# Inverting 8x8 blocks on VectorE, five weight remainders by accumulating DMA, and inputs laid out by transfer

## The chip, the cores and the metric

The kernel runs on one core of one Trainium2 chip. The metric is the device time of one execution in microseconds; the kernel before takes 667.52 us, the median of 3 runs (667.09 to 667.53).

## The reference

Two decoder layers on 256 tokens of width 1024, and a final RMSNorm, all in float32. Layer 0 has a mixer with one input projection, whose columns go to a gated-DeltaNet part (8 heads of 64, with a causal convolution of width 4 and SiLU on q, k, v) and to a short gated convolution part (512 channels, `y = Bg * conv3(Cg * h)`); one output projection follows, then a squared-ReLU MLP of width 4096. Layer 1 has a sparse attention mixer and the same kind of MLP. Every sublayer begins with an RMSNorm.

The delta rule works on chunks of 64 tokens. What matters here is its triangular solve:

```python
m_low = jnp.where(strict, jnp.einsum('nbhik,nbhjk->nbhij', kb, kc) * decay, 0.0)
a_mat = m_low + jnp.eye(c, dtype=f32)
u = lax.linalg.triangular_solve(a_mat, vc * bc[..., None], left_side=True, lower=True, unit_diagonal=True)
w = lax.linalg.triangular_solve(a_mat, kb * jnp.exp(gc)[..., None], left_side=True, lower=True, unit_diagonal=True)
```

So for each head and each chunk of 64 tokens the inverse of a 64x64 unit lower triangular matrix is wanted.

## The kernel before, in words

**Order.** The instructions of each engine stand in a fixed order, written out when the kernel is built. The class `Order` (from line 166) runs all parts of the kernel as generators ("streams") against a list of costs for each operation; whichever stream could start first, and on a tie has the lower priority number, emits next. Each engine and the DMA queue (`SP`) then execute their lists in order, with semaphores between them. Eight PSUM banks are handed out by the same planner; the projections (`MAIN`, priority 9) take a bank only when two are free. When operations are added, taken away or moved, the whole order behind them is planned anew.

**Weights.** Projections run at full float32 accuracy by splitting each weight into a rounded part and a remainder, and each activation likewise, with three float32r matmuls for one product (`mm256`). Weights come in units of up to 128x1024. `loads` (line 491) issues all transfers from memory on SP's queue into eight staging slots (`st`); `splits` (line 511) makes of unit i the rounded part `uh` on ScalarE and the remainder `ul = st - uh` on VectorE, each into one of four buffers (`UB = 4`). For the units listed in `BYDMA` (line 37), ScalarE instead writes `-uh` into `ul`, and GpSimd issues a DMA that adds `st` to it (`refill`, line 534); the planner counts 4500 ns for its landing (`DLAT`). The units are numbered: 0 to 7 for K, 8 to 15 for z and the decay inputs, 16 to 19 V, 20 to 23 Q, 24 to 27 CG (the gate Cg), 28 to 31 h, 32 to 35 Bg, 36 to 43 the output projection of layer 0.

**Layer 0.** TensorE runs the projections in that order; a group of four column blocks accumulates in PSUM and is read when its time comes: K and V through a convolution on VectorE, Q through one on GpSimd (`pool_conv`), CG after GpSimd has made `r2` (the row scale squared, `cg_evac`), h through a second convolution on GpSimd. Meanwhile `chain_k` computes the norms of k and calls `invert` (line 1271).

**The inversion.** Tokens stand in two chunks `c` of 128, that is, four blocks of 32 tokens on the partitions, for 8 heads. `prepare(c)` computes `al` (the lower triangle with its sign changed, transposed: 128 x 8 heads x 128). From it `prepare` transposes the four 32x32 diagonal blocks to `lc`, masks the entries of 2-blocks into `tt`, adds the identity, and transposes that to `uc`: the inverses of the 2x2 blocks. `invert` then doubles the block size in four levels (2, 4, 8, 16; masks in `lvl`). A level has `left` (128 matmuls of 32x32 from `al` and `tt`), a product with the mask to `ys` on VectorE, `right` (128 matmuls from `uc` and `ys`), an addition to `tt` and a transpose to `uc` on VectorE:

```python
for l in range(1, 5):
    bs, blocks = yield from left(0)
    ...
    bs = yield from right(blocks)
```

A last step of another form joins 32-blocks to 64-blocks (`U64`). Then `chain_main` solves, and `output` leads to `ya`, the half of the output projection's input that comes from the heads; `yb` is the half from the short convolution.

**The front.** `loads` issues first the 40 columns of norm weights (`wn`, 160 bytes on each partition), then x in five pieces between the first weight pieces, and later the other parameters (`par`, before weight piece 8). x and the parameters stand in memory row by row, one row per partition; each transfer takes a part of every row. The first RMSNorm (`start`, line 909) waits for a piece of x and for `wn`.

Of the kernel before, what the change touches and what calls it, by code (L numbers as in the profile page):

```python
# [20 lines left out]
T = 256  # L21
KT = D // 128
FF = 4096
NEG = -1e30
EPS = 1e-6
CH = 4096
UN = 1024
XBIAS, DBIAS, XB0 = 300, -400, 1e9
GM, GT, GO = 2, 1, 1
HEAD, CL = 0, 0  # L30
STORE, GST = (0, 2, 4, 6, 7, 8), (2,)
FIRST, XS = (1,) * 8, ((1, 2), (2, 4), (4, 6), (6, 8))
PK, PW, PR, F1, GZ, ZP, LD, RT, P2 = 1, 1, 1, 1, 1, 1, 1, 21, 8
KPOOL, VPOOL, QPOOL, CVB = (), (), (0, 1, 2, 3), {'conv': 4, 'pool': 2}
TAP = {'V': 290}
CHAIN, EARLY, TOK_FIRST = 0, 16, False
BYDMA, DLAT = (*range(113, 121, 2), *range(129, 141, 2)), 4500
YIELD = (0.0, 0.0, 0.0)
TICK, BUSY = 10240 / 3, 1500.0
FULL, DRAIN, BARE, STAY, LEAVE = (128, 128), 0.0, 0.0, 0.0, 0.0  # L40
# [20 lines left out]
    return [(UN // 2, FIRST), (528, (1,) * 8)] + [w] * 7 + [w] * 16 + l1 + [w] * 16  # L61


def _layout(i):

    ev = i['ev_w_in'][0]
    od = i['od_w_in'][0]
# [41 lines left out]
    for k in ORDER1:  # L109
# [3 lines left out]
    par = {}  # L113
    col = lambda v: v.reshape(-1, 128).T
    rep = lambda v: np.broadcast_to(v.reshape(1, -1), (128, v.size))
    par['wn'] = np.concatenate([col(v) for v in (i['mix_norm'][0], i['mlp_norm'][0], i['mix_norm'][1],
                                                 i['mlp_norm'][1], i['final_norm'])], axis=1)
# [7 lines left out]
    par['strict'] = (r[:, None] > r[None, :])  # L125
    b, c = np.arange(128) % 32, np.arange(32)
    par['lvl'] = np.concatenate([((b[:, None] // s) % 2 == 1) & (c[None, :] // s == b[:, None] // s - 1)
                                 for s in (1, 2, 4, 8, 16)], axis=1)
    par['i32'] = b[:, None] == c[None, :]
    par['onorm'] = rep(i['ev_o_norm'][0])  # L130
    par['sctap'] = i['ev_sc_conv'][0].reshape(3, 4, 128).transpose(2, 1, 0).reshape(128, 12)
    inv = np.float32(500000.0) ** (-np.arange(0, 16, 2, dtype=np.float32) / np.float32(16))
# [15 lines left out]
    for k, v in par.items():  # L148
# [1 line left out]
        off[k] = (o, v.shape[1])  # L150
        o += v.shape[1]
        parts.append(v)
    xt = i['x'][0].reshape(T, KT, 128).transpose(2, 1, 0).reshape(128, KT * T)
# [7 lines left out]
    return c32(np.concatenate(flat)), c32(xt), c32(np.concatenate(parts, axis=1)), off  # L161

# [3 lines left out]
class Order:  # L166
# [29 lines left out]
    def flag(self, name):  # L196
        self.flags.setdefault(name, self._now())
# [212 lines left out]
def _build(ctx, nc, tc, wts, xin, parin, out, off):  # L410
# [15 lines left out]

    npar = off['rc'][0]
    par = const.tile([128, npar], F32, name="par")
    X = e.X = const.tile([128, KT, T], F32, name="X")
    e.rtab = const.tile([128, 2, T], F32, name="rtab")  # L430
    ones = const.tile([128, 1], F32, name="ones")

    e.zeros = const.tile([128, 512], BF16, name="zeros")

    def keep(bank):
# [44 lines left out]
    def get(dst, src, k, name):  # L480
# [2 lines left out]
        order.spend('D', k * 512 / 330)  # L483
        flag(name)

    def load_x(a, b):
        yield from get(X[:, a:b], xin[:, a * T:b * T].rearrange("p (k t) -> p k t", t=T), (b - a) * T, f'x{a}')
        for m in range(a + 1, b):
            flag(f'x{m}')

    def loads():
        cut = off['ident'][0]
        before = {P2: [get(par[:, cut:], parin[:, cut:npar], npar - cut, 'par2')],
                  RT: [get(e.rtab, parin[:, npar:].rearrange("p (a t) -> p a t", a=2), 2 * T, 'rtab')]}
        for p, x in zip((1, 2, 3, 4), XS):
            before[p] = [load_x(*x)]
        head = [get(par[:, :cut], parin[:, :cut], cut, 'par'), load_x(0, 1)]
        before[HEAD] = head + before.get(HEAD, [])
        for p, (pos, k) in enumerate(pieces):
            for g in before.get(p, ()):  # L500
                yield from g
            slot, o = place[p]
            if not o:
                if slot >= SB:
                    yield 'flag', f'st{slot - SB}'
                st = stage.tile([128, UN], F32, name="st")
            staged[p] = st[:, o:]
            yield from get(st[:, o:o + k], bass.AP(tensor=wts.tensor, offset=wts.offset + pos, ap=[[k, 128], [1, k]]),
                           k, f'ld{p}')

    def splits(first):
        for i in range(first, len(units), 2):
# [278 lines left out]
    class Norm:  # L791


        def __init__(self, idx, last=False):
            self.idx, self.last = idx, last
            self.w = par[:, off['wn'][0] + 8 * idx:off['wn'][0] + 8 * idx + 8]
            self.x = self.acc = None
            self.begun = self.count = self.sums = 0

# [100 lines left out]
    def main():  # L900
        n0 = Norm(0)

        def root():

            yield 'flag', 'norm3'
            yield 'A'
            A.activation(tmp.tile([128, 1], F32, name="tb", bufs=3), ones, AF.Sqrt)

        def start(m):
            yield 'flag', f'x{m}'  # L910
            yield 'flag', 'par'
# [24 lines left out]
        for i, (a, b) in enumerate(zip(STORE, STORE[1:])):  # L936
            spawn(store(i, a, b))
# [55 lines left out]
def layer0(e, n, nxt):  # L993
# [4 lines left out]
    with ExitStack() as ctx:  # L998
# [253 lines left out]
        def prepare(c):  # L1252

            al = AL[c]
            yield from keys(c)
            yield from scores(c, KB, al)
            tt, lc, uc, ys = (p1.tile([128, 8, 32], F32, name=f"{k}{c}", tag=f"lz{c}" if k == "lc" else f"{k}{c}")
                              for k in ("tt", "lc", "uc", "ys"))
            yield 'V'
            for b in range(4):  # L1260
                r = slice(32 * b, 32 * b + 32)
                V.transpose(lc[r], al[r, :, r])
            V.tensor_mul(tt, lc, b32(lvl[:, 0]))
            V.tensor_add(tt, tt, b32(P('i32')))
            V.transpose(uc, tt)
            parts[c] = al, tt, uc, ys
            flag(f'parts{c}')

        parts = [None, None]

        def invert():
# [2 lines left out]
                spawn(prepare(c))  # L1274
            for c in range(2):
                yield 'flag', f'parts{c}'

            def left(shift):
                bs = yield from banks(2)
# [18 lines left out]
                                      start=True, stop=True, tile_position=(i, i))  # L1298
                return bs

            for l in range(1, 5):
                bs, blocks = yield from left(0)
                yield 'V'
                for c in range(2):
                    V.tensor_mul(parts[c][3], view(bs[c], 8, 32), b32(lvl[:, l]))
                    release(bs[c])
                bs = yield from right(blocks)
                yield 'V'
                for c in range(2):
# [777 lines left out]
```

## Time and profile before

| | |
|---|---|
| median of 3 runs | 667.52 us |
| the profiled execution's own time | 666.4 us |
| its span, first to last instruction | 664.6 us |
| mean granted TensorE clock | 0.991 |
| TensorE matmuls busy | 646.4 us (97%), 6642 instructions |
| VectorE busy | 474.0 us (71%), 911 |
| ScalarE busy | 375.4 us (56%), 715 |
| GpSimd busy | 127.5 us (19%), 167 |

PE is TensorE's matmuls, PEld its weight loads, DVE VectorE, ACT ScalarE, POOL GpSimd, SP the queue that issues transfers. Times in rows are in us from the start of the span, mean durations of one instruction in ns. Matmuls overlap each other, so the sum of their durations is more than their time; the distance between starts tells what one costs. Nearly all instructions carry the line of a helper (329), so groups are told apart by their tiles: `b` is a PSUM bank, `x` the normed input, `uh` and `ul` a weight unit's two parts, `st` its staging slot. A bracket at the end of a row holds the time for which the engine stood idle before it, and what ended that.

### The profile page before, as it was taken

To read this page: it belongs to the slowest core of one execution; us is meant where nothing else is said; L and a number is where in the kernel's file an instruction comes from. 1 tells how busy PE (TensorE), PEld (TensorE's weight loads), DVE (VectorE), ACT (ScalarE), POOL (GpSimd) and SP (SyncE) were. 2 spreads that over 40 slices of the span, in tenths; PEclk is the share of its full clock that TensorE was granted. 3 is DMA by queue.
4 is the path that set the end of the run, shared out by engine and by line. 5 is a ranking of instruction groups with operands and counts; after the bars stand their busy time and mean duration, and the time that the engine had idled before them with its cause. 6 is when DMAs were issued, how large, how long until landed. Compare 5 with 4: busy or idle time off the path is not lost.

```text
span 664.6 us, 16204 instructions
## 1 busy us (share of the span) xinstructions
PE 646.4 (97%) x6642; PEld 621.1 (93%) x6644; DVE 474.0 (71%) x911; ACT 375.4 (56%) x715; POOL 127.5 (19%) x167
## 2 busy tenths in 40 slices
PE   8999989999999999999999999999999999999995
PEld 6999878999999999999999887898999999999994
DVE  5999868876887776555557998986778777545441
ACT  7566223344676665444447689888567666544430
POOL 1101696300200000111124433120220000012121
PEclk8999989999999999999999999999999999999998
DMA  8862433245566666666667659552656555555401
GB/s 289 309 225 83 135 101 97 64 125 163 177 200 193 191 193 196 195 193 197 196 185 165 199 179 321 147 156 67 184 184 204 192 192 190 193 194 196 148 1 65
DMA packets 33915, 114.34 MB, mean 172 GB/s; under 512 B 3888, under 2 KB 4400, under 8 KB 33840
## 3 DMA queue, kind: packets, MB, share of 16 engines
q1 hardware_dynamic: 32112, 107.66, 50.8%
q0 software_dynamic: 1440, 5.24, 4.1%
q8 instruction: 52, 0.85, 0.5%
q10 hardware_dynamic: 288, 0.39, 0.2%
q14 instruction: 23, 0.19, 0.1%
HBM read 106.99 MB, written 1.05 MB: 163 GB/s over the span
## 4 chain that ended last, share of the span: by engine, by line
PE 83%; DVE 9%; ACT 2%; issue 2%; DMA 2%; SPq 0%; POOLq 0%; DVEq 0%; ACTq 0%
PE b L329 83%; DVE ul L329 3%; DVE cvconv L329 2%; ACT uh L329 1%; DMA X<-xt 1%; DMA ul<-st 1%; DVE rqt L329 1%; DVE al L329 1%; DVE lc L329 1%; ACT ul L329 0%; DVE preconv L329 0%; SPq L482 0%; DVE r L329 0%; DVE kst L329 0%; DVE tt L329 0%
## 5 line engine op out<-in xcount | busy, mean ns | idle before, releaser
L329 ACT ACTIVATE uh<-st 128x1024 fp32r<-128x1024 f32 (+3 forms) x204 | 206.2, 1012 | 205.4 <-PE b L329 170.9
L329 DVE TENSOR_TENSOR ul<-st,uh 128x1024 fp32r<-128x1024 f32 (+3 forms) x194 | 229.5, 1185 | 118.0 <-ACT uh L329 117.5
L329 PE MATMUL b<-x,uh 128*128 128x256 f32 x1664 | 294.7, 281 | 1.8 <-ACT uh L329 1.4
L329 PEld LDWEIGHTS b<-x,uh 128*128 128x128 f32 x1664 | 253.3, 189 | 3.8 <-ACT uh L329 1.9
L329 PE MATMUL b<-x,ul 128*128 128x256 f32 x832 | 232.3, 279 | 2.2 <-DVE ul L329 0.9
L329 PE MATMUL b<-U,uh 128*128 128x256 f32 x1024 | 174.2, 276 | 0.0
L329 PEld LDWEIGHTS b<-x,ul 128*128 128x128 f32 x832 | 157.5, 189 | 3.6 <-DVE ul L329 1.8
L329 PEld LDWEIGHTS b<-U,uh 128*128 128x128 f32 x1024 | 154.1, 188 | 0.0
L329 PE MATMUL b<-U,ul 128*128 128x256 f32 x512 | 141.3, 276 | 0.0
L329 PEld LDWEIGHTS b<-U,ul 128*128 128x128 f32 x512 | 96.1, 188 | 0.0
L329 POOL TENSOR_TENSOR nacc<-nacc,sq 128x256 f32<-128x256 f32 x24 | 32.0, 1334 | 234.4 <-ACT sq L329 224.8
L329 DVE SCALAR_TENSOR_TENSOR t<-b,rbc 128x256 f32<-128x256 f32 x64 | 26.6, 423 | 8.3 <-PE b L329 8.3
L329 ACT ACTIVATE U<-u 128x256 fp32r<-128x256 f32 x64 | 26.8, 419 | 2.0
L329 ACT ACTIVATE px<-b,nm 128x256 f32<-128x256 f32 (+1 forms) x64 | 26.3, 423 | 2.0 <-DVE nm L329 1.7
L329 DVE TENSOR_TENSOR U<-u,U 128x256 fp32r<-128x256 f32 x64 | 26.5, 419 | 0.0
L329 ACT ACTIVATE u<-t 128x256 f32<-128x256 f32 x64 | 25.6, 401 | 0.0
L329 DVE TENSOR_TENSOR X<-X,b 128x256 f32<-128x256 f32 (+1 forms) x28 | 13.9, 514 | 16.3 <-PE b L329 16.3
L329 POOL TENSOR_TENSOR X<-X,par 128x256 f32<-128x256 f32 x8 | 5.6, 702 | 100.3 <-ACT nacc L329 91.7
L329 PE MATMUL b<-uh,x 128*128 128x264 f32 (+1 forms) x128 | 24.7, 289 | 0.0
L329 PE MATMUL b<-ohl,uh 128*128 128x256 f32 x128 | 23.9, 287 | 0.2
L329 PEld LDWEIGHTS b<-uh,x 128*128 128x128 f32 x128 | 20.3, 188 | 0.2 <-issue 0.2
L329 PEld LDWEIGHTS b<-ohl,uh 128*128 128x128 f32 x128 | 19.6, 188 | 0.7 <-ACT ohl L329 0.3
(276 smaller groups left out, 772.3 us busy)
## 6 DMA issues: line engine op xcount, KB each, us to landing
st<-wts SPq DMA_DIRECT2D x188, 512.0 KB, 4.1
ul<-st POOLq DMA_DIRECT2D x10, 512.0 KB, 5.1
st<-wts SPq DMA_DIRECT2D x8, 280.0 KB, 3.3
st<-wts SPq DMA_DIRECT2D x8, 264.0 KB, 5.9
st<-wts SPq DMA_DIRECT2D x8, 256.0 KB, 6.3
X<-xt SPq DMA_DIRECT2D x3, 256.0 KB, 6.3
par<-par SPq DMA_DIRECT2D x1, 525.0 KB, 5.8
out_dram<-X SPq DMA_DIRECT2D x2, 256.0 KB, 2.8
```

The lines of the kernel that those rows point to most:

```text
L329: r = f(*a, **k)
```

## The change

**Inversion.** The mask table `lvl` keeps only levels 8 and 16. `prepare` no longer transposes and masks for 2-blocks; it multiplies the four 32x32 blocks of `al` by a mask of the upper part of 8-blocks (`up8`) and sums over the four block columns to `W8`, so that each row holds its 8 entries within its own 8-block. When both chunks are there, `eights` runs a substitution on VectorE over 16 heads at once: six steps, each a shuffle that brings row i of every 8-block to all its rows, a product and an addition; then it adds the identity, spreads the 8 columns to 32 with the mask `own8` into `uc`, and transposes to `tt`. Levels 8 and 16 and all behind them are as before.

**Remainders.** Units 21, 23, 25, 27 and 29 are added to `BYDMA`.

**Inputs.** x, with `wn` in front of its first piece, and the two parts of the parameters are stored so that each transfer reads one contiguous range. The norm weights come with the first piece of x (296 columns), their own transfer falls away, and `start` does not wait for it. A tile `gap0` keeps the addresses of the others.

```diff
-BYDMA, DLAT = (*range(113, 121, 2), *range(129, 141, 2)), 4500
+BYDMA, DLAT = (*range(21, 31, 2), *range(113, 121, 2), *range(129, 141, 2)), 4500
...
+def xcuts():
+    return [(0, WN + T)] + [(WN + a * T, WN + b * T) for a, b in XS]
...
-                                 for s in (1, 2, 4, 8, 16)], axis=1)
-    par['i32'] = b[:, None] == c[None, :]
+                                 for s in (8, 16)], axis=1)
+    own = b[:, None] // 8 == c[None, :] // 8
+    par['own8'] = own
+    par['up8'] = own & (c[None, :] > b[:, None])
+    par['i8'] = b[:, None] % 8 == c[None, :8]
...
+    def rows(src, at, n):
+        return bass.AP(tensor=src.tensor, offset=src.offset + 128 * at, ap=[[n, 128], [1, n]])
     def load_x(a, b):
-        yield from get(X[:, a:b], xin[:, a * T:b * T].rearrange("p (k t) -> p k t", t=T), (b - a) * T, f'x{a}')
-        for m in range(a + 1, b):
+        yield from get(xw[:, a:b], rows(xin, a, b - a), b - a, f'x{max(0, a - WN) // T}')
+        for m in range((a - WN) // T + 1, (b - WN) // T):
             flag(f'x{m}')
...
-        head = [get(par[:, :cut], parin[:, :cut], cut, 'par'), load_x(0, 1)]
-        before[HEAD] = head + before.get(HEAD, [])
...
         def start(m):
             yield 'flag', f'x{m}'
-            yield 'flag', 'par'
...
             for b in range(4):
                 r = slice(32 * b, 32 * b + 32)
-                V.transpose(lc[r], al[r, :, r])
-            V.tensor_mul(tt, lc, b32(lvl[:, 0]))
-            V.tensor_add(tt, tt, b32(P('i32')))
-            V.transpose(uc, tt)
+                V.tensor_mul(md[r], al[r, :, r], P('up8')[r, None, :].to_broadcast([32, 8, 32]))
+            V.tensor_reduce(W8[:, c], md.rearrange("p h (b c) -> p h c b", c=8), axis=AX.X, op=OP.add)
...
+        def eights():
+            W = W8.rearrange("p c h i -> p (c h) i")
+            for i in range(6, 0, -1):
+                yield 'V'
+                B = p2.tile([128, 16, 8], F32, name="b8")[:, :, i + 1:]
+                V.stream_shuffle(B, W[:, :, i + 1:], [p // 8 * 8 + i for p in range(32)])
+                V.tensor_mul(B, B, W[:, :, i:i + 1].to_broadcast([128, 16, 7 - i]))
+                V.tensor_add(W[:, :, i + 1:], W[:, :, i + 1:], B)
+            yield 'V'
+            V.tensor_add(W, W, P('i8')[:, None, :].to_broadcast([128, 16, 8]))
+            for c in range(2):
+                yield 'V'
+                _, tt, uc, _ = parts[c]
+                V.tensor_mul(uc.rearrange("p h (b i) -> p h b i", i=8), W8[:, c, :, None, :].to_broadcast([128, 8, 4, 8]),
+                             P('own8').rearrange("p (b i) -> p b i", i=8)[:, None].to_broadcast([128, 8, 4, 8]))
+                V.transpose(tt, uc)
...
+            yield from eights()
...
-            for l in range(1, 5):
+            for l in range(2):
```

More of the change, by code (lines that the diff above doesn't have):

```diff
@@ L24 @@
 NEG = -1e30
+WN = 40
 EPS = 1e-6
@@ L29 @@
 GM, GT, GO = 2, 1, 1
-HEAD, CL = 0, 0
+CL = 0
 STORE, GST = (0, 2, 4, 6, 7, 8), (2,)
@@ L115, in _layout @@
     rep = lambda v: np.broadcast_to(v.reshape(1, -1), (128, v.size))
-    par['wn'] = np.concatenate([col(v) for v in (i['mix_norm'][0], i['mlp_norm'][0], i['mix_norm'][1],
-                                                 i['mlp_norm'][1], i['final_norm'])], axis=1)
+    wn = np.concatenate([col(v) for v in (i['mix_norm'][0], i['mlp_norm'][0], i['mix_norm'][1],
+                                          i['mlp_norm'][1], i['final_norm'])], axis=1)
     par['ident'] = np.eye(128)
@@ L152, in _layout @@
         parts.append(v)
-    xt = i['x'][0].reshape(T, KT, 128).transpose(2, 1, 0).reshape(128, KT * T)
+    xt = np.concatenate([wn, i['x'][0].reshape(T, KT, 128).transpose(2, 1, 0).reshape(128, KT * T)], axis=1)
+    xt = [np.ravel(xt[:, a:b]) for a, b in xcuts()]
     c32 = lambda a: np.ascontiguousarray(a, dtype=np.float32)
@@ L160, in _layout @@
             c = c[:, k:]
-    return c32(np.concatenate(flat)), c32(xt), c32(np.concatenate(parts, axis=1)), off
+    par = np.concatenate(parts, axis=1)
+    o = off['rc'][0]
+    par = np.concatenate([np.ravel(par[:, :o]), np.ravel(par[:, o:])])
+    return c32(np.concatenate(flat)), c32(np.concatenate(xt)), c32(par), off
 class Order:
@@ L428, in _build @@
     par = const.tile([128, npar], F32, name="par")
-    X = e.X = const.tile([128, KT, T], F32, name="X")
+    xw = const.tile([128, WN + KT * T], F32, name="X")
+    X = e.X = xw[:, WN:].rearrange("p (k t) -> p k t", t=T)
     e.rtab = const.tile([128, 2, T], F32, name="rtab")
     ones = const.tile([128, 1], F32, name="ones")
+    const.tile([128, 56], F32, name="gap0")
     e.zeros = const.tile([128, 512], BF16, name="zeros")
@@ L484, in get @@
         flag(name)
+    def rows(src, at, n):
+        return bass.AP(tensor=src.tensor, offset=src.offset + 128 * at, ap=[[n, 128], [1, n]])
     def load_x(a, b):
-        yield from get(X[:, a:b], xin[:, a * T:b * T].rearrange("p (k t) -> p k t", t=T), (b - a) * T, f'x{a}')
-        for m in range(a + 1, b):
+        yield from get(xw[:, a:b], rows(xin, a, b - a), b - a, f'x{max(0, a - WN) // T}')
+        for m in range((a - WN) // T + 1, (b - WN) // T):
             flag(f'x{m}')
     def loads():
[L492 to L495, printed above, removed]
+        before = {P2: [get(par, rows(parin, 0, npar), npar, 'par2')],
+                  RT: [get(e.rtab.rearrange("p a t -> p (a t)"), rows(parin, npar, 2 * T), 2 * T, 'rtab')]}
+        for p, x in enumerate(xcuts()):
             before[p] = [load_x(*x)]
-        head = [get(par[:, :cut], parin[:, :cut], cut, 'par'), load_x(0, 1)]
-        before[HEAD] = head + before.get(HEAD, [])
         for p, (pos, k) in enumerate(pieces):
@@ L507, in loads @@
             staged[p] = st[:, o:]
-            yield from get(st[:, o:o + k], bass.AP(tensor=wts.tensor, offset=wts.offset + pos, ap=[[k, 128], [1, k]]),
-                           k, f'ld{p}')
+            yield from get(st[:, o:o + k], rows(wts, pos // 128, k), k, f'ld{p}')
     def splits(first):
@@ L795, in __init__ @@
             self.idx, self.last = idx, last
-            self.w = par[:, off['wn'][0] + 8 * idx:off['wn'][0] + 8 * idx + 8]
+            self.w = xw[:, 8 * idx:8 * idx + 8]
             self.x = self.acc = None
@@ L1256, in prepare @@
             yield from scores(c, KB, al)
-            tt, lc, uc, ys = (p1.tile([128, 8, 32], F32, name=f"{k}{c}", tag=f"lz{c}" if k == "lc" else f"{k}{c}")
-                              for k in ("tt", "lc", "uc", "ys"))
+            tt, md, uc, ys = (p1.tile([128, 8, 32], F32, name=f"{k}{c}", tag=f"lz{c}" if k == "md" else f"{k}{c}")
+                              for k in ("tt", "md", "uc", "ys"))
             yield 'V'
@@ L1261, in prepare @@
                 r = slice(32 * b, 32 * b + 32)
-                V.transpose(lc[r], al[r, :, r])
-            V.tensor_mul(tt, lc, b32(lvl[:, 0]))
-            V.tensor_add(tt, tt, b32(P('i32')))
-            V.transpose(uc, tt)
+                V.tensor_mul(md[r], al[r, :, r], P('up8')[r, None, :].to_broadcast([32, 8, 32]))
+            V.tensor_reduce(W8[:, c], md.rearrange("p h (b c) -> p h c b", c=8), axis=AX.X, op=OP.add)
             parts[c] = al, tt, uc, ys
             flag(f'parts{c}')
+        W8 = small("w8", 2, 8, 8)
+        def eights():
[14 more added lines that the diff above has]
+                V.transpose(tt, uc)
         parts = [None, None]
```

## The prediction

> **What bounds the kernel now.** I read the page's busy times first, then the chain that ended last, then busy time by stretch.
>
> ```profile
> span 664.6 us, 16204 instructions
> PE 646.4 (97%) x6642; PEld 621.1 (93%) x6644; DVE 474.0 (71%) x911; ACT 375.4 (56%) x715; POOL 127.5 (19%) x167
> ...
> PE 83%; DVE 9%; ACT 2%; issue 2%; DMA 2%; SPq 0%; POOLq 0%; DVEq 0%; ACTq 0%
> ```
>
> TensorE is busy 97% of the span and carries 83% of the chain, so time is gained where TensorE has less to do, stands still, or runs at a lower clock. The change lies in layer 0, ahead of the MLP that begins at 176.9 us (last row, from the chain in order of time). Its stretches (columns: PE, PEld, DVE, ACT, POOL busy with instructions; granted clock; DMA share, GB/s):
>
> ```profile
> 5.30:9.20 3.90, 3.57 (x25) 2.97 (x24) 2.16 (x4) 1.71 (x5) 0.00 (x0) 1.00 0.87 256
> 9.20:10.50 1.30, 0.00 (x0) 0.00 (x0) 0.88 (x2) 1.30 (x4) 0.00 (x0) 1.00 1.06 407
> 10.50:15.00 4.50, 4.24 (x20) 4.04 (x21) 4.38 (x10) 4.50 (x12) 0.00 (x0) 0.62 1.04 405
> ...
> 54.70:68.60 13.90, 13.90 (x128) 13.77 (x131) 13.61 (x35) 7.20 (x10) 2.15 (x2) 1.00 0.37 106
> 68.60:106.50 37.90, 34.32 (x1202) 32.17 (x1202) 28.72 (x55) 10.21 (x16) 32.13 (x41) 0.95 0.38 118
> 106.50:141.60 35.10, 34.01 (x495) 31.79 (x495) 27.94 (x66) 12.00 (x21) 10.46 (x14) 1.00 0.26 77
> ...
> 176.88 175.68 PE b L329 x1547
> ```
>
> Up to 68.6 us VectorE is almost full (13.61 of 13.90) but TensorE is full too, so VectorE costs nothing there. From 68.6 to 106.5, where the inversion runs, TensorE loses 37.90 - 34.32 = 3.6 us standing still, and the clock of 0.95 takes 5% of 37.9, about 1.9 us. After that it is nearly full again. The MLP and layer 1 behind are untouched, so what layer 0 gives goes to the end one for one.
>
> **The inversion on TensorE.** Each of four levels issues two batches of 128 small matmuls (2 chunks x 8 heads x 4 blocks):
>
> ```profile
> 68.53 1.31 PE L329 MATMUL b<-tt,al 32*32 32x32 f32 x128
> 69.77 0.50 PE L329 MATMUL b<-x,uh 128*128 128x256 f32 x2
> ...
> 72.56 1.31 PE L329 MATMUL b<-ys,uc 32*32 32x32 f32 x128 [1.10 <-DVE ys L329]
> ...
> 84.12 1.54 PE L329 MATMUL b<-tt,al 32*32 32x32 f32 x128
> ...
> 92.19 0.25 PE L329 MATMUL b<-ys,uc 32*32 32x32 f32 x4 [1.78 <-issue]
> ```
>
> From the start of a batch to the next matmul is 69.77 - 68.53 = 1.24 us. The change leaves levels 8 and 16, so four batches go: **-4.96 us** of TensorE work. The standing and slow clock above (3.6 + 1.9 = 5.5 us) belong to four levels; two go, but the worst stop (1.78) sits in a level that stays, so I take less than half: **-2.3 us**, bounds 0 and -5.5.
>
> **The inversion on VectorE.** Rows grouped by shape:
>
> ```profile
> L329 DVE STREAM_TRANSPOSE uc<-tt 128x256 f32<-128x256 f32 x10 | 4.5, 446 | 0.3
> L329 DVE STREAM_TRANSPOSE lc<-al 32x256 f32<-32x256 f32 x8 | 3.5, 434 | 0.1
> L329 DVE TENSOR_TENSOR tt<-tt,b 128x256 f32<-128x256 f32 x8 | 3.2, 402 | 2.0 <-PE b L329 2.0
> L329 DVE TENSOR_TENSOR ys<-b,par 128x256 f32<-128x256 f32 x8 | 3.0, 412 | 0.0
> L329 DVE TENSOR_TENSOR tt<-lc,par 128x256 f32<-128x256 f32 x2 | 0.9, 426 | 0.1
> L329 DVE SCALAR_TENSOR_TENSOR lq<-lq,lw 128x16 f32<-128x16 f32 x5 | 0.9, 175 | 0.2
> ```
>
> Removed: 8 transposes to lc (3.5), four operations on tt at 0.43 (1.7), two uc (0.9), and of two levels four each of ys, tt and uc (1.65 + 1.6 + 1.8): 11.1 us. Added: eight products md, 32x256 like the lc transposes (3.5); two reductions of 256 elements, taken like a tt operation (0.8); six steps of shuffle, product and sum on 16 to 96 elements; an addition of 128; two products and two transposes of 256 (1.7). For the small ones the nearest row is 128x16 at 0.175, with 256 elements at 0.43: (0.43 - 0.175)/240 = 1.06 ns an element. The sizes 16, 32, ... 96 exceed 16 by 240 in all, so three kinds cost 3 x (6 x 0.175 + 0.25) = 3.9 us, and the addition 0.3. If every small one cost 0.43 it would be 8.0. Added 10.2 us (bounds 10 to 15), net about -1. Since VectorE runs beside full projection matmuls this is priced at nothing; that cover gone (nothing else for TensorE while the six steps run), it is up to 6 us. The chain itself gets shorter: two levels ran from 68.53 to 84.12, 15.6 us, and about 6 us takes their place.
>
> **Five remainders by DMA.** Units 21, 23 hold blocks of Q, 25 and 27 of CG, 29 of h. VectorE loses 5 x 1.30 us; ScalarE gets 5 negated copies of 1.06 us, GpSimd 5 issues, and readiness comes later. An existing unit of this kind, in order of time on ScalarE, GpSimd, and the chain:
>
> ```profile
> L329 DVE TENSOR_TENSOR ul<-st,uh 128x1024 fp32r<-128x1024 f32 x36 | 46.4, 1296 | 10.2 <-ACT uh L329 10.1
> ...
> 364.89 1.07 ACT L329 ACTIVATE uh<-st 128x1024 fp32r<-128x1024 f32 x1
> 366.12 1.05 ACT L329 ACTIVATE ul<-uh 128x1024 fp32r<-128x1024 f32 x1
> ...
> 367.46 5.55 DMA ul<-st
> ...
> L329 POOL DMA_DIRECT2D ul<-st x10: 855/874/1024, 348.9 to 471.1; - x10
> DMA to landing us min/median/max: 4.4/5.1/9.1
> ```
>
> From the start of uh to landed this is 373.01 - 364.89 = 8.1 us. How much lead is there? Where only projections run, ScalarE's copies follow TensorE's release of buffers:
>
> ```profile
> 61.04 1.06 ACT L329 ACTIVATE uh<-st 128x1024 fp32r<-128x1024 f32 x1 [1.66 <-PE b L329]
> 63.76 1.06 ACT L329 ACTIVATE uh<-st 128x1024 fp32r<-128x1024 f32 x1 [1.66 <-PE b L329]
> 66.53 1.06 ACT L329 ACTIVATE uh<-st 128x1024 fp32r<-128x1024 f32 x1 [1.71 <-PE b L329]
> ...
> 80.14 1.04 ACT L329 ACTIVATE uh<-st 128x1024 fp32r<-128x1024 f32 x1
> ...
> L329 PE MATMUL b<-x,uh 128*128 128x256 f32 x104 | 20.8, 299 | 0.3 <-DVE ys L329 0.3
> L329 PE MATMUL b<-x,ul 128*128 128x256 f32 x52 | 15.2, 292 | 0.4 <-issue 0.4
> ...
> 71.85 0.78 POOL L329 TENSOR_TENSOR cvpool<-prepool,par 128x256 f32<-128x256 f32 x1 [14.36 <-DVE prepool L329]
> ...
> 93.55 0.61 POOL L329 TENSOR_TENSOR r<-rbc 128x256 f32<-128x256 f32 x1
> ```
>
> A unit lasts 2.72 us, and with four buffers one is filled three units ahead: 3 x 2.72 = 8.2 us. So 8.1 just fits where TensorE does nothing but projections; where the small work is mixed in (104 + 52 projection matmuls between 68.6 and 106.5, 24 to a unit: 6.5 units in 37.9 us, 5.8 us a unit) the lead is 17 us. A late unit stops TensorE, whose order is fixed, and with it the small matmuls of the inversion queued behind. Counted back from the output projection's first unit, the copies at 61.04, 66.53 and 80.14 are units 25, 27 and 29. So four of the five DMAs are issued while GpSimd is idle, before its first convolution at 71.85; only unit 29's stands in its queue ahead of the convolutions of Q and of CG x h, 0.9 us later for ScalarE's SiLU of Q, whose norms have until the inversion is done. VectorE's copy of that unit slowed GpSimd by as much when the two met, so I leave it at nothing. ScalarE is busy 7.20 of 13.90 and then 10.21 of 37.90; its five copies (5.3 us) fit in. SP's next loads wait for a staging slot until the accumulation has landed, some 5 us later; with eight slots of 2.72 us they are 21 us ahead: nothing, and up to 5 us where that lead is used up. I price the five at **+1.0 us**, a quarter of a microsecond for each in the full stretch; bounds 0 and, at the longest landing of 9.1, 12.1 - 8.2 = 3.9 for each of four, 15.6.
>
> By the Trainium skill, "DMA: Bandwidth & Descriptors" (Anatomy of one DMA), a software-issued transfer takes about 2.0 us plus its bytes over 436 GB/s; an estimate for 512 KB is 3.2 us. The trace's 5.1 median differs and decides; by the page the +1.0 would be 0, and the time 659.8.
>
> **The inputs.** The norm weights go along with the first block of x, one transfer fewer ahead of everything:
>
> ```profile
> 0.74 0.38 SPq L482 DMA_DIRECT2D par<-par  x1
> 1.18 0.42 SPq L482 DMA_DIRECT2D X<-xt  x1
> ...
> 9.06 0.91 ACT L329 ACTIVATE x<-X,par 128x256 fp32r<-128x256 f32 x2 [1.79 <-DMA X<-xt]
> ```
>
> All later issues on SP's queue move up by 1.18 - 0.74 = **-0.44 us**, and the front waits for a landing (9.06), so it counts. The other parameters stay at their place in the queue. That rows of x now follow one another in memory has no row of its own; bounds: 0, and what the front loses, 1.30 standing plus (1 - 0.62) x 4.5 = 1.7 of slow clock, -3.0. The first is nearer, as the width of a partition's row stays. The Trainium skill says the same, "Perfetto Trace Analysis" (Contiguity and DMAs): contiguity matters only within a partition's line. Against it stands that 5.3 to 9.2 us moved 256 GB/s at a share of 0.87, and the next stretch 407 at 1.06; by that row there may be up to 3 us in it, the third rival.
>
> **Sum:** -4.96 - 2.3 + 1.0 - 0.44 = -6.7 us. The profiled execution took 666.4 us (span 664.6 and 1.8 around it), so 659.7; the median of the runs lies 667.5 - 666.4 = 1.1 higher, so **660.8 us**.
>
> **Rivals.** (1) *Another bound takes the batches' place.* The accumulators of CG cannot be read until GpSimd, at the end of Q's convolution, has made r (71.85 to 93.55 in the rows above). If they and Q's accumulators fill the eight PSUM banks, projections cannot run ahead in the freed 5 us and TensorE stands instead; then only the front and 0.7 of stops remain: 667.5 - 1.1 = 666.4. For it: GpSimd is busy 32.13 of 37.90. Against: fewer batches also hold fewer banks. (2) *Slower: the landings are late.* Without the four batches between them units 25 and 27 too are taken at 2.72 us, so four units have a lead of 8.2 us. TensorE stops at each until the accumulation is there; from 7.7/4 = 1.9 us each (a landing of 7 us) the gain is gone, and at two thirds of the bound the five are 10.4 us: 667.5 + 10.4 - 7.7 = 670.2. For it: SP's loads fill 0.37 and 0.38 of the DMA engines at the same time, and 9.1 has occurred. Against: the median of 5.1, and that unit 21's copy is made long before its use. (3) *More: the front also loses its stop and its slow clock*, 660.8 - 3.0 = 657.8.
>
> **Chances.** Forecast 0.54 (own range 658.5 to 663.5), rival 1 0.18, rival 2 0.13, rival 3 0.15. A measurement tells 0.2% (1.3 us) from no change. Faster: 0.54 + 0.15 + 0.07 of rival 1 = 0.76; within: 0.11; slower: 0.13. The range reaches to rivals 1 and 3: 656.5 to 667.0.
>
> **What would show it.** Right: 512 small matmuls less; the stretch from the first batch to the end of the inversion is shorter by about 13 us; the MLP begins near 170 us. Wrong: "DMA ul" above 2 us among TensorE's waits before 100 us (rival 2); TensorE's standing between 68 and 106 us grown past 6 us with r still near 93 (rival 1); the third x landing over 1 us sooner beyond the shift (rival 3). The forecast falls if the MLP begins later than 174 us.

## The result, and the profile after

The changed kernel takes 656.7 us (median of four runs, 654.6 to 658.5) against 667.3 us (666.6 to 667.5) for the kernel before in the same comparison: a ratio of 0.984, 95% interval 0.981 to 0.986. That is 10.6 us less; the forecast was 660.8. Its own range, 658.5 to 663.5, does not hold the time; the wide one, 656.5 to 667.0, holds it at its lower edge. The profiled execution is the fastest of the four, 654.6 us with a span of 652.8. Its mean granted clock is 0.999, that of the other three 0.995 to 0.997, so its rows show the least slow clock of the four.

The page of the changed kernel (busy time, share of the span, instructions):

```profile
span 652.8 us, 15211 instructions
PE 638.1 (98%) x6132; PEld 613.3 (94%) x6132; DVE 470.3 (72%) x919; ACT 380.7 (58%) x720; POOL 132.1 (20%) x172
...
PE 83%; DVE 6%; ACT 4%; issue 3%; DMA 3%; POOL 0%; SPq 0%; DVEq 0%; POOLq 0%; ACTq 0%
```

TensorE has 510 recorded matmuls less and is still the bound. Busy time by stretch, changed kernel (columns as in the prediction), and from its chain of waits the row with which the MLP begins:

```profile
5.30:9.20 3.90, 3.85 (x27) 3.40 (x26) 2.64 (x7) 2.62 (x7) 0.00 (x0) 1.00 0.96 337
9.20:10.50 1.30, 1.07 (x8) 0.87 (x9) 1.20 (x3) 1.30 (x5) 0.00 (x0) 1.00 1.06 407
10.50:15.00 4.50, 4.26 (x35) 3.86 (x34) 4.50 (x11) 4.50 (x13) 0.98 (x1) 1.00 1.04 408
...
54.70:68.60 13.90, 13.54 (x120) 13.34 (x118) 13.55 (x37) 8.74 (x10) 3.29 (x5) 1.00 0.74 172
...
79.22:95.12 15.90, 13.24 (x571) 12.23 (x571) 9.53 (x21) 3.31 (x5) 14.22 (x20) 1.00 0.53 175
95.12:130.33 35.21, 34.39 (x507) 32.37 (x505) 31.13 (x71) 14.73 (x26) 20.64 (x26) 1.00 0.25 77
68.60:106.50 37.90, 34.81 (x882) 33.01 (x883) 29.49 (x63) 14.80 (x23) 27.47 (x36) 1.00 0.56 164
```

```profile
164.91 175.72 PE b L343 x1547
```

The MLP begins at 164.9 us instead of 176.9, 12.0 us sooner, and the span is 11.8 shorter: all of the gain is made ahead of the MLP, and nothing behind it (1547 matmuls in 175.7 us on both sides). The granted clock is 1.00 in every one of these stretches; before it was 0.62 in 10.5 to 15.0 and 0.95 in 68.6 to 106.5. In 68.6 to 106.5 TensorE stands 37.90 - 34.81 = 3.1 us, before 3.6.

TensorE's waits of the changed kernel from 52 to 165 us, and its batches of small matmuls in order of time:

```profile
PE b L343 <- issue: 2.6, 3, 1.3
PE b L343 <- DVE r L343: 0.8, 1, 0.8
PE b L343 <- DMA ul<-st: 0.8, 1, 0.8
```

```profile
79.22 1.51 PE L343 MATMUL b<-tt,al 32*32 32x32 f32 x128
82.30 1.06 PE L343 MATMUL b<-ys,uc 32*32 32x32 f32 x98
84.50 0.45 PE L343 MATMUL b<-ys,uc 32*32 32x32 f32 x30 [1.13 <-issue]
87.17 0.89 PE L343 MATMUL b<-tt,al 32*32 32x32 f32 x80
89.32 0.61 PE L343 MATMUL b<-tt,al 32*32 32x32 f32 x48 [1.27 <-issue]
...
92.17 0.74 PE L343 MATMUL b<-ys,uc 32*32 32x32 f32 x62
93.15 0.80 PE L343 MATMUL b<-ys,uc 32*32 32x32 f32 x66 [0.24 <-issue]
```

Four batches are left, the first 10.7 us later than before. What TensorE still waits for most has no engine's name: "issue" inside three of the four. Keep the numbers 98, 30, 80, 48, 62 in mind; with the 18 projection matmuls that lie between the second batch and the third, and again between the third and the fourth, they are the clue to the stops.

### The profile page after: what moved, and what is told of

It is laid out like the page before. It is cut to its first block, busy times and chain, and to the rows that moved or that the text cites. A ratio compares the mean times of both kernels' runs of the same rounds, so it can differ in the third digit from the quotient of the medians.

```text
span 652.8 us, 15211 instructions
## 1 busy us (share of the span) xinstructions
PE 638.1 (98%) x6132; PEld 613.3 (94%) x6132; DVE 470.3 (72%) x919; ACT 380.7 (58%) x720; POOL 132.1 (20%) x172
## 4 chain that ended last, share of the span: by engine, by line
PE 83%; DVE 6%; ACT 4%; issue 3%; DMA 3%; POOL 0%; SPq 0%; DVEq 0%; POOLq 0%; ACTq 0%
PE b L343 82%; DVE ul L343 2%; DMA ul<-st 1%; ACT uh L343 1%; DMA st<-wts 1%; DMA X<-xt 1%; DVE cvconv L343 1%; ACT E L343 1%; ACT ul L343 1%; DVE rqt L343 0%; ACT KD L343 0%; DVE kst L343 0%; DVE nacc L343 0%; DVE KL L343 0%; SPq L498 0%
## 5 line engine op out<-in xcount | busy, mean ns | idle before, releaser
L343 DVE TENSOR_TENSOR ul<-st,uh 128x1024 fp32r<-128x1024 f32 (+3 forms) x189 | 222.5, 1179 | 118.6 <-ACT uh L343 118.2
L343 PE MATMUL b<-x,uh 128*128 128x256 f32 x1664 | 291.3, 279 | 0.2
L343 POOL DMA_DIRECT2D ul<-st x15 | 13.2, 879 | 72.4 <-DVE sp L343 25.0
L343 POOL TENSOR_TENSOR X<-X 128x256 f32<-128x256 f32 x8 | 5.6, 702 | 100.3 <-ACT nacc L343 91.7
```

The source lines that it names most:

```text
L343: r = f(*a, **k)
```

## The experiments

The table has all runs: the median, the ratio to the kernel before with its interval, and of the profiled execution the start of the MLP, TensorE's standing between 52 and 164 us (length less busy time of the stretches 52 to 110 and 110 to 164) and what the lower clock took there (busy time x (1 - granted clock)), in us. The kernel before had a median of 666.7 to 667.3 in the comparisons. The last three columns are of one execution each: it lies 2.1 us below the median for changed, 3.7 below for inv_dma, and 1.1 below for before.

| kernel | median | ratio | MLP at | standing | slow clock |
|---|---|---|---|---|---|
| before | 667.3 | | 176.9 | 5.7 | 1.6 |
| changed | 656.7 | 0.984 (0.981 to 0.986) | 164.9 | 4.4 | 0 |
| inputs_only | 665.4 | 0.998 (0.997 to 0.999) | 175.9 | 6.1 | 1.6 |
| merge_only | 665.6 | 0.997 (0.996 to 0.999) | 176.9 | 5.9 | 3.2 |
| inv_only | 670.2 | 1.005 (1.003 to 1.006) | 179.9 | 10.5 | 6.9 |
| dma_only | 669.9 | 1.005 (1.002 to 1.007) | 178.3 | 5.9 | 3.2 |
| inv_dma | 657.3 | 0.985 (0.983 to 0.987) | 164.6 | 3.0 | 0 |
| after_no_dma | 669.0 | 1.003 (1.001 to 1.004) | 179.3 | 11.0 | 7.4 |
| inv_lean | 659.8 | 0.988 (0.987 to 0.990) | 170.4 | 4.8 | 3.2 |
| before_lean | 664.2 | 0.995 (0.994 to 0.997) | 175.7 | 3.8 | 3.3 |
| after_lean | 659.1 | 0.987 (0.986 to 0.989) | 170.0 | 5.7 | 3.3 |
| inv_first | 660.8 | 0.990 (0.987 to 0.993) | 173.7 | 6.0 | 4.8 |
| inv_last | 670.0 | 1.004 (1.003 to 1.006) | 179.0 | 11.5 | 4.5 |
| after_twice | 670.3 | 1.005 (1.003 to 1.007) | 184.1 | 14.8 | 5.6 |
| after_split | 664.6 | 0.996 (0.995 to 0.998) | 175.6 | 9.9 | 4.5 |
| after_shift | 657.2 (one run) | | 168.3 | 5.9 | 1.6 |
| before_shift | 667.7 | 1.001 (0.999 to 1.002) | 177.3 | 6.6 | 1.6 |

Take the start of the MLP less the two columns behind it: it is 160.5 to 163.0 in the kernels with the new inversion (163.7 with its doubled batches) and 167.8 to 169.5 in those with the old. So the kernels fall into two narrow groups, some 7 us apart, and most of what else tells them from one another is standing and slow clock. What the front loses before 52 us is still in these numbers. TensorE's busy time at full clock up to the MLP, which leaves it out, is 164.0 us in the kernel before, 157.9 in the changed one and 161.9 in after_twice, which executes as many matmuls as the kernel before.

### Each part alone, and two together

```diff
 # inputs_only: only the layout of x, parameters and norm weights
 # inv_only: only the masks, prepare, eights and range(2) for the levels
 # dma_only: only
-BYDMA, DLAT = (*range(113, 121, 2), *range(129, 141, 2)), 4500
+BYDMA, DLAT = (*range(21, 31, 2), *range(113, 121, 2), *range(129, 141, 2)), 4500
 # inv_dma: inv_only and dma_only, the inputs as before
```

> The kernel before with the input layout and the norm weights in the first piece of x, nothing else. Theory A (the extra gain over the forecast is the front: one issue less and earlier landings, and with them the stop of 1.3 us and the slow clock behind it): -2.0 us in the first 52 us, third piece of x at about 7.6 us rather than 9.06, median 664 to 665. Theory B (the extra gain is made in the inversion's stretch, by the order planned anew): only the issue of 0.44 us, 666.5 to 667.

> The kernel before with the 8-blocks on VectorE, nothing else. Theory A: four batches less, -5 us, and half the stops, -2: about 660.5. Theory B (CG's accumulators hold the banks until r is made behind Q's convolution, and only the DMA units move r forward): the batches' time turns into stops, r stays above 90 us, -1 to -3: 664.5 to 666.5.

> The kernel before with units 21 to 29 (odd) by accumulating DMA, nothing else. Theory A: no gain, 0 to +1.5, for TensorE did not wait for VectorE there: 667.5 to 669. Theory B: GpSimd's order changes and r comes before Q's convolution, so the slow clock and stops of the inversion's stretch fall: -2 to -4, 663.5 to 665.5.

> The changed kernel with the inputs as before. Theory A: it lacks the front's 2 us, so 658.5 to 659.5. Theory B: it has all but 0.44 us of the gain, about 657.

The inputs gave 1.1 us; the inversion alone cost 3.2 and the DMA remainders alone 3.0; the two together gave 10.2, as much as the whole change to within the scatter. Neither theory had said that two parts that are each a loss make the gain: +3.2 + 3.0 is 16.4 us away from -10.2. Where each loses, from 52 to 110 us, in the rows of before, inv_only, dma_only and inv_dma, in this order:

```profile
52.00:110.00 58.00, 54.16 (x1441) 51.53 (x1439) 48.09 (x100) 21.76 (x37) 35.06 (x44) 0.97 0.34 103
```

```profile
52.00:110.00 58.00, 48.77 (x892) 46.81 (x894) 43.89 (x109) 19.51 (x31) 30.17 (x42) 0.89 0.34 102
```

```profile
52.00:110.00 58.00, 53.23 (x1367) 50.93 (x1366) 38.85 (x93) 23.73 (x33) 29.42 (x40) 0.94 0.53 142
```

```profile
52.00:110.00 58.00, 56.13 (x1096) 53.78 (x1096) 50.28 (x119) 28.87 (x42) 37.72 (x47) 1.00 0.59 171
```

TensorE stands 9.2 us in inv_only, and runs at a clock of 0.89; in dma_only it stands 4.8 at 0.94, while VectorE, 38.85 busy of 58, has room that nobody uses; in inv_dma it stands 1.9 at full clock. Whom it waits for in inv_only, 52 to 165 us, and where:

```profile
PE b L332 <- DVE bv L332: 4.6, 2, 2.6
PE b L332 <- ACT lsq L332: 3.2, 1, 3.2
PE b L332 <- ACT Vf L332: 1.0, 1, 1.0
```

```profile
75.54 0.33 PE L332 MATMUL b<-par,Vf 128*128 128x128 f32 x1 [0.98 <-ACT Vf L332]
77.84 0.66 PE L332 MATMUL b<-par,Vf 128*128 128x128 f32 x4 [1.96 <-DVE bv L332]
81.14 1.93 PE L332 MATMUL b<-tt,al 32*32 32x32 f32 x128 [2.65 <-DVE bv L332]
```

And VectorE's work just ahead of that, inv_only in order of time:

```profile
73.80 0.29 DVE L332 STREAM_SHUFFLE b<-w 128x80 f32<-128x80 f32 x1
74.13 0.24 DVE L332 TENSOR_TENSOR b<-b,w 128x80 f32<-128x80 f32 x1
74.40 0.24 DVE L332 TENSOR_TENSOR w<-w,b 128x80 f32<-128x80 f32 x1
74.56 0.48 DVE L332 SCALAR_TENSOR_TENSOR cvconv<-preconv,par,cvconv 128x256 f32<-128x256 f32 x1
...
75.76 1.22 DVE L332 TENSOR_TENSOR ul<-st,uh 128x1024 fp32r<-128x1024 f32 x1
76.89 0.28 DVE L332 TENSOR_TENSOR w<-w,par 128x128 f32<-128x128 f32 x1
77.10 0.68 DVE L332 TENSOR_TENSOR bv<-b,beta 128x512 f32<-128x512 f32 x1
```

VectorE does three things by turns: the steps of the 8-blocks, the convolution of V (cvconv), and a remainder (ul) of 1.22 us about every 2.8 us. The last of V's convolution ends at 75.0, so TensorE's transposes of V stand at 74.5 us, and behind them, in the fixed order, the first batch (at 81.14). V's lateness goes on to Q: its accumulators are read from 81.0 (in the changed kernel from 69.5), GpSimd's convolution starts at 81.5 (70.0), and TensorE stands 3.2 us more, at 101.5, for the norms of Q. TensorE's slow clock behind both stops is the third loss.

### Is it VectorE's room, or the DMA as such?

```diff
-            lo = unitp.tile([128, UN + 64], F32R, name=f"ul{i % UB}")[:, :UN]
+            lo = hi if i in LEAN else unitp.tile([128, UN + 64], F32R, name=f"ul{i % UB}")[:, :UN]
...
-            if i in BYDMA:
+            if i in LEAN:
+                split_done(i)
+            elif i in BYDMA:
...
+LEAN = range(21, 31, 2)
```

With this edit in inv_only, in the kernel before and in the changed one, the five remainders are not made at all.

> The 8-blocks on VectorE as in the change, the inputs as before, and no accumulating DMA: the remainders of the five pieces 21, 23, 25, 27 and 29 are left out altogether (the products with them take the rounded weights a second time, so TensorE does the same number of matmuls). So VectorE gets the 5 x 1.14 us back that the DMA gave it, but nothing is put on a DMA queue. Theory C (the inversion on VectorE is worth its matmuls only where VectorE has room between 55 and 80 us; the DMA is the means): about 657, 10 us under the kernel before, with the MLP's first norm near 165 us and no TensorE wait over 1 us behind VectorE in 70 to 82 us. Theory D (the DMA's own lateness re-orders the work and that order is the lucky one): 664 or more, with the 6 us of waits that the inversion alone had at 74 to 81 us still there.

> The kernel before with the remainders of the same five pieces left out (the products take the rounded weights twice): VectorE's relief without DMA traffic and without the change's inversion. The five DMA remainders alone had cost 3.0 us. Theory C (relief has no buyer while TensorE itself bounds the stretch): between 664.5 and 668, about the kernel before. Theory D (any new order of this stretch is worse by luck): about 670 again, with the same stops. Theory E (the 2.6 MB that the accumulating DMA moves delay the 16 KB pages of TensorE's instructions, and so lengthen the stops inside the batches of small matmuls): 665 or less, with under 3 us of such stops against 4.3 in the kernel with the five DMA remainders alone.

> The changed kernel with the remainders of the five pieces left out instead of made by DMA: what the DMA path itself costs in the changed kernel. The prediction priced it at 1.0 us (bounds 0 to 15.6). Theory C: 655 to 657, within 1.5 us of the changed kernel, the 0.8 us wait for a late remainder gone. Theory E (instruction pages delayed by the traffic): 653 to 655, with the stops of 1.13 and 1.27 us inside the batches under 0.6 us each. Theory D: away from the changed kernel by more than 3 us on the slow side.

inv_lean: 659.8, 10.4 us under inv_only without a byte of that DMA, and no wait behind VectorE above 0.4 us from 70 to 82. (The edit also spares TensorE any wait for these remainders, but inv_only had none of those.) So VectorE's room carries most of what the five remainders gave the inversion (12.9 us by inv_dma). It is short of the 657 expected: this kernel has stops of 1.06 and 1.51 us "issue" in and behind its second batch and one of 1.62 behind ScalarE at 140 us, and lost 3.2 us to the clock. In the kernel before, leaving the remainders out gave 3.1, a little more than theory C allowed, where the DMA had cost 3.0; theory E (DMA traffic delays instructions) fits that, with 2.8 us of stops without a name against 4.3 in dma_only, but falls with after_lean, which is 2.4 us slower than the changed kernel although it moves less by DMA: its stops in and behind the second batch are 1.68 and 2.21 us. Part of theory D is therefore true: with a new order the stops change, and with them 2 to 3 us. Why the DMA remainders alone cost 3.0 stays open; the runs of that kernel also lie furthest apart, 665.5 to 673.0.

```diff
 # inv_only, and
-BYDMA, DLAT = (*range(113, 121, 2), *range(129, 141, 2)), 4500
+BYDMA, DLAT = (*range(21, 27, 2), *range(113, 121, 2), *range(129, 141, 2)), 4500    # inv_first
+BYDMA, DLAT = (*range(25, 31, 2), *range(113, 121, 2), *range(129, 141, 2)), 4500    # inv_last
 # after_no_dma: the changed kernel with the old BYDMA
```

> The 8-blocks on VectorE with three of the five DMA remainders (21, 23 and 25), the inputs as before. The inversion alone had cost 3.2 us, with all five it gave 10.2. Theory C (VectorE's room is what decides): three fifths of the relief, between 659 and 664, with the wait behind VectorE at 74 to 82 us down from 5.6 to under 3 us. Theory D (only the order of the whole set is the lucky one): 666 or more. If the first three pieces, which VectorE meets before 70 us, are all that is needed: 656 to 658.5.

> The inversion with the last three of the five DMA remainders (25, 27 and 29) instead of the first three, the inputs as before. With the first three it took 660.8. If any three give VectorE the room: 659 to 662.5, no wait behind VectorE over 1.5 us from 70 to 85 us. If the room is wanted early, before the last evacuations of V at 75 us: 664 to 669, with 3 to 5 us of waits behind VectorE left there.

> The changed kernel without the five DMA remainders: the inputs and the inversion together. Theory C (VectorE has no room for the 8-blocks without them): the inversion's +3.2 and the inputs' -1.1, about 669 (667 to 671), with over 4 us of waits behind VectorE between 70 and 85 us. If the inputs gave VectorE the room instead: under 662.

The first three remainders bring 9.4 of the 12.9 us, the last three nothing: VectorE's room is wanted before about 75 us, not somewhere. In inv_last ScalarE takes up V's last convolution earlier than in inv_only (68.7 us against 75.1), but Q comes no better off: TensorE waits 2.10 us for an evacuation of Q (prepool) in the middle of its first batch and 4.07 us for Q's norms. That is more than was expected, and so is the time (670.0, expected 664 to 669):

```profile
83.66 0.75 PE L332 MATMUL b<-tt,al 32*32 32x32 f32 x64 [2.10 <-DVE prepool L332]
97.04 1.01 PE L332 MATMUL b<-par,lsq 128*128 128x2 f32 x4 [4.07 <-ACT lsq L332]
```

after_no_dma came out as the sum of its parts said, 669.0.

### What the stops without a name are

One queue, q8, carries packets of instructions of 16 KB each: 52 in the kernel before, which has 6642 matmuls, and 48 in the changed one, which has 6132 (packets, MB, share):

```profile
q8 instruction: 52, 0.85, 0.5%
```

```profile
q8 instruction: 48, 0.79, 0.5%
```

That is one packet for every 128 matmuls with their weight loads, and a batch is exactly 128. In the changed kernel the cuts lie 30 + 18 + 80 = 128 and 48 + 18 + 62 = 128 matmuls apart. So theory F: the stops are instruction pages that have not come.

```diff
 # after_shift (before_shift the same): behind the warm-up
+        for _ in range(64):
+            PE.eng.matmul(b[:32, :32], w[:32, :32], w[:32, :32], start=True, stop=True)
 # after_twice: each batch of the two levels once more, onto the same results
+                if not shift:
+                    for c in range(2):
+                        ...
+                                PE.eng.matmul(view(bs[c], 8, 32)[i:i + 32, h], al[j:j + 32, h, i:i + 32], tt[j:j + 32, h],
+                                          start=True, stop=True, tile_position=(j, i))
+                ...
 # after_split: between the two halves of such a batch
+                    if c and not shift:
+                        order.later(1500)
+                        yield SMALL
```

> The changed kernel with 64 very small matmuls on zeros added behind the warm-up at the start, where TensorE stands anyway: 128 instructions, half a page of 16 KB, and nothing else moved. Theory F: the places of the stops move by 64 matmuls to the front; the second batch, which was cut 98 to 30, is cut 34 to 94, the third, cut 80 to 48, is cut 16 to 112, and the stops keep their length to within 0.5 us; time 655 to 659. Theory P (something in the batches themselves): the cuts stay at 98 and 80.

> The changed kernel with each of its four batches of 128 small matmuls (the two rounds of the inversion on four blocks of 32) issued twice over, the second time onto the same results; everything else in its order. Theory P (a batch costs its 1.24 us of TensorE, as the prediction had it): 4 x 1.24 = 5.0 us more, about 661.7. Theory F (TensorE's instructions come in pages of 16 KB, 256 instructions, so a batch with its 128 weight loads is a whole page; in the changed kernel a stop inside a batch ended 4.2 us after the page before had been entered, so a page takes about that long to come): four pages more, 4 x 4.2 = 17 us less what stood there anyway (2.6 us), and lower granted clock behind stops that are over 1.5 us: 668 to 680, with stops of 2 us or more in every batch for which the profile names no other engine.

> The changed kernel with 1.5 us of other work let in between the two halves of each of those four batches (the order is planned anew with that pause in the inversion's chain), so that about 13 more projection matmuls lie between one batch of 128 and the next. Theory F: a page then lasts 1.24 + 30 x 0.114 = 4.6 us, longer than the 4.2 us that the next takes to come, and the stops of 1.13, 1.27 and 0.24 us go: 654 to 656.5, no stop without a named cause over 0.5 us from 78 to 102 us. Theory P (the stops are the price of going over to the 32-row shape): twice as many changes of shape, the stops stay or grow, 657 to 660. Rival to both: the chain's end comes 6 us later and holds up what needs the inverse: 659 or more with a wait behind VectorE or ScalarE after 100 us.

> The kernel before with the 64 very small matmuls on zeros behind the warm-up (half an instruction page), and nothing else moved. Theory F (instruction pages): the batch that was cut 124 to 4 by a stop of 1.78 us is cut 60 to 68, the stop of 0.43 us among the projections before it goes into a batch too, and the time moves by what the stops and the lower clock behind them become, at most 3 us either way: 664.5 to 670. Theory P: the cut stays at 124 to 4 and the time within 0.7 us of the kernel before.

The batches of after_shift:

```profile
82.65 0.50 PE L343 MATMUL b<-ys,uc 32*32 32x32 f32 x34
83.82 1.02 PE L343 MATMUL b<-ys,uc 32*32 32x32 f32 x94 [0.67 <-issue]
87.04 0.33 PE L343 MATMUL b<-tt,al 32*32 32x32 f32 x16
88.37 1.17 PE L343 MATMUL b<-tt,al 32*32 32x32 f32 x112 [1.00 <-issue]
...
92.35 1.30 PE L343 MATMUL b<-ys,uc 32*32 32x32 f32 x126
95.65 0.24 PE L343 MATMUL b<-ys,uc 32*32 32x32 f32 x2 [2.00 <-issue]
```

Half a page added at the start moves the cuts from 98 to 34 and from 80 to 16, the very numbers expected. Nothing in the batches themselves does that: the stops are instruction pages. The trace shows it directly too, for it has the time of each packet. In the changed kernel packets of q8 are on their way from 82.0 to 82.9, from 86.9 to 87.9 and from 90.8 to 91.7 us, and the stops end at 84.50, 89.32 and 93.15, each time about 1.5 us after a landing. So it is in the other kernels: each of the 35 stops on "issue" in all of them between 52 and 130 us ends 0.8 to 1.6 us after a packet of q8 has landed. One thing was not expected: the last cut, 62 with 0.24 us, became 126 with 2.00, and the clock fell behind it.

before_shift moved its cut too (124 to 4 became 120 to 8, three batches sooner, with 2.01 us), though not to the place that I had worked out; the time is that of the kernel before. There too the two stops lie a page apart, 8 transposes of V and 120 small matmuls, where the kernel before has 4 projections and 124.

after_twice: 512 small matmuls more cost 13.6 us, 3.4 us for a batch instead of 1.24; its stops were 0.97, 4.35, 2.07, 1.93, 0.82 and 2.44 us. That is theory F's figure (668 to 680), though the one stop of the third batch stays just under the 2 us expected of every batch. after_split did what it should to the stops (one of 1.30 is left of three) and lost elsewhere: TensorE waits 1.88 us for a late remainder at 82.3, the inversion ends later, the last projection of x is done at 115 us (in the changed kernel at 127), and TensorE stands 3.3 us up to 148.5 for VectorE's o, which nothing covers. The rival named there happened, and the version is no improvement.

Behind a long stop the clock goes down. dma_only, in order of time:

```profile
73.67 0.87 PE L329 MATMUL b<-tt,al 32*32 32x32 f32 x78
76.37 0.64 PE L329 MATMUL b<-tt,al 32*32 32x32 f32 x50 [1.83 <-issue]
76.94 0.51 PE L329 MATMUL b<-x,uh 128*128 128x256 f32 x2
...
78.34 0.63 PE L329 MATMUL b<-x,uh 128*128 128x256 f32 x2
```

Two projection matmuls take 0.63 instead of 0.39 us for the next 3 us. In the profiled executions, all nine kernels whose longest stop without a name was 1.51 to 2.33 us, in or next to their batches, lost 1.6 to 3.3 us to the clock between 52 and 110; the changed kernel (1.27 at most) and inv_dma (1.01) lost none. The loss comes in steps of about 1.6 us: the granted clock goes to 0.50 for some 3.3 us, or for twice that. But the length of one stop does not decide alone. In before_lean the clock also fell behind stops of 0.35 and 0.83 us within 2 us, in inv_first behind 1.22, 0.16 and 0.40 within 3.5 us, while in after_twice it did not fall behind one of 1.93.

### The inputs

```diff
 # merge_only: the norm weights ahead of x's first piece, rows strided as before
-            yield from get(X[:, a:b], xin[:, a * T:b * T].rearrange("p (k t) -> p k t", t=T), (b - a) * T, f'x{a}')
+            yield from get(xw[:, a:b], xin[:, a:b], b - a, f'x{max(0, a - WN) // T}')
```

> The norms' weights travel in front of the first piece of x, so one DMA issue less, but rows stay strided as before; no other part of the change. Both parts of the inputs together gave 1.1 us. Theory A1 (the issue that is gone carries the gain): 665.3 to 666.2 against about 666.8 before, and the third piece of x is first used 0.9 us or more sooner than in the kernel before (8.1 us or less against 9.06). Theory A2 (the contiguous layout carries it): within 0.5 us of the kernel before, and the third piece comes only some 0.5 us sooner (8.5 us or later), with a stop of 0.8 us or more still behind it at 10 us.

The first use of the third piece of x, ScalarE, in merge_only and in the changed kernel:

```profile
7.79 0.89 ACT L336 ACTIVATE x<-X 128x256 fp32r<-128x256 f32 x2
```

```profile
7.56 0.91 ACT L343 ACTIVATE x<-X 128x256 fp32r<-128x256 f32 x2 [0.60 <-DMA X<-xt]
```

Of 9.06 - 7.56 = 1.50 us the merged transfer makes 1.27, three times the 0.44 by which the issue moves; the layout makes 0.2. Why joining two transfers brings three times one issue is not shown. The times of merge_only and inputs_only (665.6, 665.4) cannot be told apart. The layout is as good as nothing, as the rule of the Trainium skill cited in the prediction ("Perfetto Trace Analysis", Contiguity and DMAs) had it.

## Why the prediction was right, and where it was wrong

The sign and the place were right: the gain lies ahead of the MLP, and goes to the end one for one. The MLP, forecast near 170, begins 5 us sooner. From the first batch to the last result of these levels it is 15.9 us (79.2 to 95.1) where it was 35.7 (68.5 to 104.3): 20 us less, not 13. The two levels that went had 15.6 of them, and the two that stayed now take 4.2 less.

- **Four batches, -4.96.** The rows agree: those of the eight batches add up to 11.3 us, of the four left to 6.1. As a price it was too low by about 1 us: TensorE's busy time at full clock up to the MLP went down by 6.1. That is not the batches alone, for the 512 matmuls that after_twice puts back raise it by only 4.0; what the rest is stays open. A batch more costs 3.4 us where pages are short.
- **Stops and slow clock, -2.3.** This is the term that failed, with "the worst stop (1.78) sits in a level that stays, so I take less than half". A stop belongs to no level; it falls wherever the 128th matmul after the last page does, and is as long as the page is late. Standing and slow clock between 52 and 164 us, the DMA's wait included, went from 7.4 in the profile of before to 4.4 in that of the changed kernel and to 3.0 in that of inv_dma: -3.0 and -4.4, where the terms for stops and DMA made -1.3. These two executions are faster than their medians, so by the medians it is an estimate: 10.6 us less 6.1 for TensorE's work and 1.1 for the inputs leaves 3.4, which is 2.1 more than forecast and about half of the 3.9 us that the forecast missed; the batches missed 1.1, the inputs 0.7. The bound of -5.5 held it.
- **VectorE, priced at nothing.** For the change as a whole that stood; the reason given did not. It "runs beside full projection matmuls", but TensorE's fixed order waits for V and Q, which VectorE evacuates, and VectorE was already full to 68.6 us. Without the DMA remainders the same inversion costs 3.2 us, where my terms without the DMA and the inputs make -7.3. The prediction named a price of up to 6 us for a lost cover and did not see that the five remainders were the cover. The sizes: the eighteen small operations took 6.4 us in the changed kernel against 3.9 estimated; in inv_only, where GpSimd does nothing beside them, they took 4.1. All that was added to VectorE took 14.0, inside the bounds of 10 to 15.
- **Five remainders, +1.0.** TensorE waited once, 0.79 us, for a landing of 7.6 us (the five: 4.6 to 7.6, median 6.0); in after_twice and after_split single waits were 1.42 and 1.88. The bound set the longest landing, 9.1, in place of the median of 5.1, though the row added up has 5.55: it should be 3.5 for one and some 14 for four. As a cost by itself the term was about right, and as a term of the sum it was misleading: in company of the inversion they are worth 12.9 us, alone they cost 3.0. The sum treated as separate what only works together.
- **Inputs, -0.44.** Measured -1.1 (interval 0.4 to 1.8) alone. Rival 3's mark, the third landing over 1 us sooner beyond the shift, is met at 1.06, and the stop of 1.30 is gone; but inv_dma without the inputs is as fast to within the scatter. The slow clock at 10.5 to 15 us is missing in the profiles of seven other kernels with the old inputs, so its loss is not the inputs' gain.
- **Rivals 1 and 2** did not come: standing from 68.6 to 106.5 was 3.1 us, not over 6, and r was made at 67.3, ahead of Q's convolution, since the new order put it there; the wait for landings was 0.8 us, not over 2.

## What to carry to other kernels

Price the parts of a change together when one makes room on the engine that another fills: here each of two parts lost 3 us alone and both gained 10. When TensorE waits for nothing that has a name, count its instructions from stop to stop, and look when the packets of its instruction queue landed; if the count is constant and a packet lands shortly before each stop ends, it is the instruction supply, and work in many tiny matmuls costs more than its TensorE time. A stop that lowers the clock costs about twice itself (1.83 us and 1.6 behind it in dma_only), so a change that shortens it a little may gain more than the work that it removes.

## What the runs showed of the hardware

TensorE's instructions came in 16 KB packets, one for 128 matmuls and their weight loads. A stop ended 0.8 to 1.6 us after its packet had landed, and the packet was on its way for 0.9 to 2.4 us; the longest was in before_lean, which has none of the five transfers. When pages were used up at once, the next stop ended 3.55 to 4.82 us after the one before in the changed kernel and after_shift, and 5.65 in after_twice (from 81.34 to 86.99). So a page that takes less than about 4 us to execute (128 small matmuls and 18 projections: an estimate of 3.3 us) makes TensorE stand. The Trainium skill, "Runtime: NRT & Kernel Launch" (Instruction fetch mechanics), gives the block of 16 KiB and 256 instructions, which agrees; that crossing it is mostly hidden does not hold in these batches.

The clock fell, to half and for about 3.3 us at a time, behind most stops of 1.5 us and more, and twice behind several shorter ones close together. The Trainium skill, "TensorE: Matmul & The Clock Gate" (Part 1), puts the fall after an idle window of about 3.4 us; the rows of dma_only show it behind 1.83.

A VectorE sum of 128 x 48 took 1.41 us while GpSimd issued a DMA and made r, against 0.21 for the product of the same size just before it.
